# A causal convolution by fast algorithms on one core: H1's S rows stored in reverse, one F operation for H0, and two lists of steps in a new order

## The chip, the core and the metric

The kernel runs on one core of one Trainium2 chip. The metric is device microseconds (us) of one execution, the median of several runs; lower is better. A core has TensorE (matrix products, written PE in the profile), VectorE (DVE), ScalarE (ACT), GpSimd (POOL, which here also issues most loads) and SyncE (SP, which issues the stores and the transposing loads). The engines run their own lists of instructions in order and wait for each other through semaphores.

## What is computed

```python
def reference(x, kernel):          # x: 8 x 4096 x 512, kernel: 8 taps x 512 x 512, float32
    out = np.zeros_like(x)
    for k in range(8):
        shifted = x if k == 0 else np.concatenate([np.zeros((B, k, D)), x[:, :-k, :]], axis=1)
        out += np.matmul(shifted, kernel[k])
    return out
```

Each output row is the sum of eight products of the last eight input rows with eight 512 x 512 matrices.

## The kernel before

The 8 x 4096 rows are cut into 128 runs of 256 steps in time; the run is the partition, the step is the `t` of the code. Rows of `x` are loaded as bf16 and brought into a ring `XR` of 20 steps, with the 512 features on the partitions. The first four steps are done directly (`direct(tap, t)`, 32 products). The other 252 steps are 21 blocks of 12, and each block is done by a short convolution in two levels, which replaces products by sums of inputs and sums of weights. A block has four **nodes**, in this order: PL, MI, H1, H0. Node `n` counts from 1, so nodes 1 to 4 are the first block and node 84 is the last one. A "product" is four 128 x 128 by 128 x 512 matmuls.

A node that isn't a leaf (all but nodes 3 and 4) does this, and the names are the tokens of the order lists:

- `z`: seven rows `Z` (four for H0, which takes three over from H1), sums or differences of rows of `XR`, on DVE.
- `A`: two rows from `Z`, DVE. `s`: five rows `S` of sums of `Z` rows (four for H0), DVE. `F0`, `F1`: two rows each of `F`, sums of two `S` rows, for the two halves LO and HI, DVE.
- `a1`, `u`, `a0`: three products into the bank `q`, with a copy of `q` on ACT behind `a1`. `s0`, `s1`: ACT copies `q` into the banks of the two halves; `dt`: ACT copies the rest into the tile `DT`.
- `v0`, `v1`: one product of an `S` row into each half; `d0`, `d1`: DVE forms `DT - p` and `-p - DT` in the bank; `l00`, `l01`, `l10`, `l11`: four products of `F` rows.
- `e0`, `e1`: the half leaves PSUM into a tile `y` (pool of five) or is added to one: on ACT for PL, on DVE for the others. `ga`, `gb`, `ya`: sums of `y` tiles on POOL. `store` sends a `y` tile to DRAM through SP's queue, and a later `e` that takes the buffer waits until that store has landed.
- `x12`, `x16`, `x20`: transposing loads into `XR` (SP); `r0`, `r1`, `r2`: loads of later rows by POOL. `behind` ties a POOL operation to the DVE operation that was written last before it.

A node of H0 shares rows with H1. Its sums `S[1..4]` are written to rows 0 to 3, and `S[0]` is H1's last row, which still stands in row 4. So its two F operations read rows out of sequence: `F0` reads row 0 twice (a broadcast) and rows 1 and 4, `F1` rows 1 to 3.

The scheduler does nothing here (`manual_schedule`): each engine does its instructions in the order in which the code emits them. `ORDER` is the list for one block, a token `name.i` meaning step `name` of node `4m + i + 1` for block `m`: `.0` is PL, `.1` MI, `.2` H1, `.3` H0, `.4` and `.5` the next block's PL and MI. In front of it stands the set-up, written as some 190 calls: loads of the eight taps (`load_w`), direct products, transposes on PE (`transpose_pe`) for the first rows, filler matmuls on zeros (`fill`), the 28 sums of weights (`wsum(a, b, c)`, `plus`), each one DVE operation of 128 x 2048, and the steps of nodes 1 to 6 in an order of their own. `do` runs a step once only, so the loop over `ORDER` skips what the set-up has done.

```python
    W[a, b, c]                      # a: H1, H0, MI, PL = 0, 1, 2, 3; b, c: LO, HI, MID = 0, 1, 2
    load(W[n >> 2, n >> 1 & 1, n & 1], kr[:, :, tap, :])     # n = 7 - tap
```

In listings of instructions a weight tile reads `w211_91` for `W[MI, HI, HI]` and so on; `w3_96` is the tile of all PL weights, which first holds rows of `x`, and `w4_97` holds S and A rows of the first nodes.

Of the kernel before, what the change touches and what calls it, by code (L numbers as in the profile page):

```python
# [14 lines left out]
def kernel(  # L15
# [379 lines left out]
    def s_rows(n, a, b):  # L395
# [5 lines left out]
        d1.1 l01.1 l00.1 s.2 a0.2 x12.0 u.2 l10.1 e1.0 s0.2 e0.1 s1.2 l11.1 v0.2 z.3 F0.2 A.3 F1.2 ga0.2  # L401
        v1.2 x20.1 dt.2 a1.3 d0.2 r0.2 l01.2 e1.1 l00.2 s.3 a0.3 u.3 gb0.2 d1.2 e0.2 l10.2 E0.2 z.4 F0.3
        r1.2 A.4 l11.2 s1.3 F1.3 s0.3 v0.3 v1.3 ya0.2 r2.2 dt.3 d0.3 a1.4 l01.3 e1.2 l00.3 s.4 gb1.2 a0.4
        d1.3 e0.3 u.4 l11.3 z.5 s0.4 F0.4 A.5 s1.4 dt.4 ga1.2 v0.4 v1.4 l10.3 d0.4 a1.5 d1.4 l00.4 l01.4
        a0.5 u.5 e0.4 F1.4 e1.3 s.5 s0.5 l10.4 dt.5 s1.5 z.6 A.6 x16.4 l11.4 F0.5 v0.5 v1.5 a1.6 d0.5 F1.5
# [38 lines left out]
    nc.vector.memset(zero, 0.0)
    nc.sync.dma_start(out=XF, in_=xr[:, 0:4, :])
    cast(nc.vector.tensor_copy, 2, 4)
    make_identity(nc, ident)
    for k in range(7):
        fill(pair(2 + k % 2))
    rows(H[:, 4:8], RUN - 4, 4)  # L450
    cast(nc.scalar.copy, 0, 2)
    transpose_pe("x0", 2, xin[0], 0, 4)
    load_w(0)
    load_w(4)
    fill(pair(3))
    fill(pair(3))
    here(nc.scalar.copy, 0, "x0", 0, 2)
    transpose_pe("h4", 3, H, 4, 8)
    here(nc.scalar.copy, 0, "x0", 2, 4)
    fill(pair(2))  # L460
    history(nc.scalar.copy, -4, "h4")
    direct(0, 1)
    go(3, "v0")
    go(2, "d1")
    direct(0, 0)
    direct(0, 2)
    direct(0, 3)
    direct(4, 2)
    fill(pair(2))
    load_w(1)  # L470
    direct(4, 0)
    direct(1, 1)
    direct(1, 3)
    wsum(MI, HI, HI)
    load_w(5)
    load_w(3)
    wsum(MI, HI, LO)
    direct(1, 0)
    load_w(7)
    direct(5, 3)  # L480
    plus((HI, LO))
    wsum(MI, HI, MID)
    go(3, "F1")
    plus((HI, HI))
    plus((LO, LO))
    wsum(PL, HI, MID)
    rows(H[:, 1:4], RUN - 7, 3)
    load_w(6)
    direct(1, 2)
    direct(4, 1)  # L490
    wsum(H1, MID, LO)
    direct(3, 0)
    direct(4, 3)
    direct(3, 3)
    load_w(2)
    load_xin(4)
    direct(5, 1)
    direct(3, 1)
    wsum(H0, MID, LO)
    wsum(PL, MID, LO)  # L500
    transpose_pe("h3", 2, H, 1, 4)
    load_xin(8, 0, 2)
    go(4, "F1")
    direct(7, 3)
    wsum(MI, LO, LO)
    history(nc.scalar.copy, -7, "h3")
    direct(6, 3)
    wsum(H0, MID, HI)
    plus((LO, HI))
    direct(3, 2)  # L510
    direct(6, 2)
    direct(5, 2)
    direct(5, 0)
    direct(2, 1)
    wsum(MI, LO, HI)
    transpose_pe("x4", 3, xin[4], 0, 4)
    wsum(PL, MID, HI)
    transpose_pe("x8", 2, xin[8], 0, 2)
    direct(7, 0)
    here(nc.scalar.copy, 4, "x4", 0, 2)  # L520
    wsum(MI, LO, MID)
    wsum(PL, LO, MID)
    wsum(MI, MID, HI)
    load_xin(8, 2, 4)
    direct(2, 0)
    here(nc.scalar.copy, 8, "x8", 0, 2)
    go(3, "d1")
    wsum(PL, MID, MID)
    direct(7, 1)
    here(nc.scalar.copy, 4, "x4", 2, 4)  # L530
    fill(pair(3))
    z_rows(nodes[1], 0, 5)
    node_A(nodes[1])
    load_x(12)
    transpose_pe("x9", 2, xin[8], 2, 4)
    direct(2, 3)
    here(nc.scalar.copy, 10, "x9", 0, 2)
    s_rows(nodes[1], 0, 3)
    direct(6, 0)
    z_rows(nodes[1], 5, 7)  # L540
    node_a1(nodes[1])
    load_x(16)
    wsum(H1, MID, HI)
    s_rows(nodes[1], 3, 5)
    direct(6, 1)
    go(2, "v1")
    fill(pair(2))
    node_u(nodes[1])
    node_z(nodes[2])
    node_a0(nodes[1])  # L550
    go(1, "F1")
    node_A(nodes[2])
    direct_out(0)
    node_dts(nodes[1])
    direct(7, 2)
    node_seed(nodes[1], 0)
    node_seed(nodes[1], 1)
    wsum(MI, MID, LO)
    node_F(nodes[1], 0)
    for t in range(20, 40, 4):  # L560
        load_x(t)
    direct(2, 2)
    node_v(nodes[1], 0)
    node_d(nodes[1], 0)
    go(2, "F0")
    wsum(MI, MID, MID)
    node_a1(nodes[2])
    go(1, "s")
    node_v(nodes[1], 1)
    direct_out(1)  # L570
    go(1, "l01")
    go(1, "l00")
    node_d(nodes[1], 1)
    go(1, "e0")
    go(1, "u")
    go(1, "a0")
    transpose_x(12)
    go(1, "l10")
    go(1, "z")
    do("x16", 1)  # L580
    go(1, "l11")
    go(1, "s1")
    wsum(H1, MID, MID)
    go(1, "s0")
    go(1, "v0")
    go(1, "dt")
    go(1, "F0")
    go(1, "A")
    go(1, "d0")
    go(1, "a1")  # L590
    go(2, "F1")
    go(1, "v1")
    go(2, "l01")
    go(2, "l00")
    go(2, "a0")
    go(2, "u")
    go(1, "e1")
    go(1, "d1")
    go(2, "s0")
    go(2, "dt")  # L600
    wsum(H0, MID, MID)
    go(3, "dt")
    go(2, "s")
    go(3, "v1")
    go(2, "e0")
    go(2, "l11")
    go(2, "z")
# [95 lines left out]
```

## Time and profile before

| | |
|---|---|
| median of 3 runs (lowest, highest) | 718.1 us (717.59, 718.16) |
| span of the profiled execution | 717.2 us; the page has no other time of its own for it, so it stands 0.9 below the median |
| PE busy | 696.0 us (97%), 3205 records of matmuls |
| DVE busy | 683.3 us (95%), 767 instructions |
| ACT, POOL busy | 287.7 us (40%), 167.5 us (23%) |
| granted PE clock | 0.998 of full |
| DMA | 138.86 MB, mean 194 GB/s |

Busy time counts the union of an engine's instructions. DVE's instructions overlap by some 0.08 us (the next one starts before the recorded end of the last), so the price of one in a packed row is the distance of two starts, not its recorded duration. The same holds for matmuls of PE: recorded 379 ns, but 0.216 us apart.

### The profile page before, as it was taken

What the parts mean: (1) busy time and instruction counts of PE and PEld (TensorE: products, weight loads), DVE (VectorE), ACT (ScalarE), POOL (GpSimd) and SP (SyncE); (2) the same over time, 40 slices, a digit from 0 to 9 for tenths busy, and PEclk for the clock granted to TensorE, in tenths of its full rate; (3) what the DMA queues carried; (4) which work ended last, traced back from release to release, by engine and by line L of the source; (5) the groups of instructions that cost most, each with busy time, mean ns of one, the idle gap of its engine ahead of it and who ended that gap; (6) DMA issues with size and microseconds to landing.
All of it is one profiled execution on the core that took longest, in us unless ns stands there. A gap on an engine that the chain in (4) does not pass through costs nothing.

```text
span 717.2 us, 8960 instructions
## 1 busy us (share of the span) xinstructions
PE 696.0 (97%) x3205; PEld 315.0 (44%) x3270; DVE 683.3 (95%) x767; ACT 287.7 (40%) x448; POOL 167.5 (23%) x180
## 2 busy tenths in 40 slices
PE   7989999999999999999999999999999999999995
PEld 3444444444444444444444444444444444444442
DVE  1899999999999999999999999999999999999994
ACT  3043244343435444343443434353443434444341
POOL 4200012213131221304122131312213041221212
PEclk9999999999999999999999999999999999999999
DMA  9996988788797878879788887977788698855414
GB/s 194 209 225 139 235 156 243 158 233 181 206 226 174 233 167 231 181 189 217 182 241 158 231 184 205 229 176 229 168 237 174 189 224 178 238 119 186 157 68 175
DMA packets 159515, 138.86 MB, mean 194 GB/s; under 512 B 130160, under 2 KB 134256, under 8 KB 159344
## 3 DMA queue, kind: packets, MB, share of 16 engines
q1 hardware_dynamic: 145312, 99.37, 46.6%
q0 software_dynamic: 13728, 38.15, 31.6%
q10 hardware_dynamic: 432, 0.79, 0.3%
...
q14 instruction: 18, 0.15, 0.1%
HBM read 77.33 MB, written 99.09 MB: 246 GB/s over the span
## 4 chain that ended last, share of the span: by engine, by line
PE 84%; DVE 5%; issue 5%; DMA 0%; POOL 0%; DVEq 0%; POOLq 0%
PE pp L127 84%; DVE w L84 2%; DVE Z L84 2%; DVE y L87 1%; DVE S L84 1%; DMA out_dram<-y 0%; POOL y L311 0%; DVE y L84 0%; DVE F L84 0%; DVE pp L87 0%; DVE pp L84 0%; POOL xd L93 0%; DVEq L84 0%; DVEq L87 0%; POOLq L93 0%
## 5 line engine op out<-in xcount | busy, mean ns | idle before, releaser
L127 PE MATMUL pp<-w,F 128*128 128x512 bf16 x1285 | 310.4, 379 | 3.2 <-DVE pp L87 1.3
L127 PE MATMUL pp<-w,Z 128*128 128x512 bf16 x941 | 231.9, 379 | 2.7 <-DVE Z L84 1.7
L127 PEld LDWEIGHTS <-F 128*128 128x128 bf16 x1312 | 128.3, 98 | 157.6 <-issue 3.4
L311 POOL TENSOR_TENSOR y<-y 128x512 f32<-128x512 f32 x80 | 101.7, 1272 | 406.0 <-DVE F L84 266.1
L127 PE MATMUL pp<-w,S 128*128 128x512 bf16 x658 | 157.5, 379 | 0.7
L84 DVE TENSOR_TENSOR Z<-XR 128x2048 bf16<-128x2048 bf16 (+3 forms) x109 | 154.5, 1435 | 2.5
L127 PEld LDWEIGHTS <-Z 128*128 128x128 bf16 x960 | 92.3, 98 | 118.2 <-DVE Z L84 9.4
L198 ACT COPY pp<-pp 128x512 f32<-128x512 f32 x82 | 46.7, 570 | 221.1 <-PE pp L127 221.1
L84 DVE TENSOR_TENSOR S<-Z 128x2560 bf16<-128x2560 bf16 (+1 forms) x81 | 114.5, 1413 | 0.0
L84 DVE TENSOR_TENSOR F<-S 128x1024 bf16<-128x1024 bf16 x160 | 111.1, 694 | 1.9 <-PE pp L127 1.9
L127 PEld LDWEIGHTS <-S 128*128 128x128 bf16 x672 | 65.8, 98 | 79.4 <-issue 0.2
L214 ACT COPY pp<-pp 128x512 f32<-128x512 f32 (+1 forms) x84 | 48.9, 582 | 76.5 <-PE pp L127 76.5
...
L84 DVE TENSOR_TENSOR pp<-DT,pp 128x512 f32<-128x512 f32 x82 | 56.3, 687 | 0.2 <-PE pp L127 0.2
L87 DVE SCALAR_TENSOR_TENSOR pp<-pp,DT 128x512 f32<-128x512 f32 x82 | 56.5, 689 | 0.0
L216 ACT ACTIVATE pp<-pp 128x512 f32<-128x512 f32 (+1 forms) x84 | 50.1, 596 | 15.2 <-PE pp L127 9.8
L84 DVE TENSOR_TENSOR Z<-Z 128x1024 bf16<-128x1024 bf16 x78 | 53.4, 684 | 0.7
L87 DVE SCALAR_TENSOR_TENSOR y<-pp,y 128x1024 f32<-128x1024 f32 x42 | 51.0, 1215 | 0.0
L220 ACT COPY DT<-pp 128x512 f32<-128x512 f32 x82 | 48.9, 597 | 2.6 <-PE pp L127 2.6
L268 ACT COPY y<-pp 128x1024 f32<-128x1024 f32 x40 | 40.6, 1016 | 22.9 <-PE pp L127 21.7
L87 DVE SCALAR_TENSOR_TENSOR y<-y,pp 128x1024 f32<-128x1024 f32 (+1 forms) x41 | 48.3, 1181 | 0.3 <-PE pp L127 0.3
L270 ACT ACTIVATE y<-y 128x1024 f32<-128x1024 f32 x40 | 42.3, 1057 | 2.8 <-DMA out_dram<-y 0.6
...
## 6 DMA issues: line engine op xcount, KB each, us to landing
...
XR<-xd SPq DMA_TRANSPOSE x61, 4.8
...
```

The lines of the kernel that those rows point to most:

```text
L84: last["dve"] = nc.vector.tensor_tensor(out=o, in0=a, in1=b, op=op)
L87: last["dve"] = nc.vector.scalar_tensor_tensor(out=o, in0=a, scalar=by, in1=b, op0=MUL, op1=op)
L93: return nc.gpsimd.dma_start(out=o, in_=src)
L127: nc.tensor.matmul(bank, lhsT=comp[:, c * P:(c + 1) * P], rhs=w[:, c, :], start=start and c == 0, stop=c == DC - 1, skip_group_check=True)
L198: nc.scalar.copy(out=n.q[:, 0], in_=n.q[:, 1])
L214: nc.scalar.copy(out=o, in_=q)
L216: nc.scalar.mul(out=o, in_=q, mul=-1.0)
L220: nc.scalar.copy(out=DT, in_=n.q[:, 0])
L268: nc.scalar.copy(out=cc[b_], in_=p)
L270: nc.scalar.mul(out=dd[b_], in_=cc[b_], mul=-0.5)
L311: behind(nc.gpsimd.tensor_tensor(out=cc[b_][:, j], in0=cc[b_][:, j], in1=dd[b_][:, j], op=ADD), b_ > j and n.k)
```

## The change

- A node of H1 that isn't a leaf writes its five `S` rows in reverse (`n.s[:, ::-1]`), so its first sum lies in row 4 and its last in row 0. H0 now writes its four sums to rows 1 to 4, and `S[0]`, H1's last, stands in row 0: its five rows lie in sequence.
- `F0` and `F1` of H0 become one operation `F` of four rows. `comps` names the rows that the products read, so that each product reads what it read before.
- The list `ORDER` is written anew, and the set-up is one list of tokens, `SETUP`, that reaches to node 9 and has the loads, sums, fillers and steps in a new order. The count of matmuls is as before (3168 of 128 x 512 for the products, 26 fillers, 76 transposes); DVE has 21 instructions fewer.

```diff
     def node_s(n):
+        z, o = n.z, n.o
         if n.shares:
-            tt(n.s[:, 0:4], n.z[:, n.o + 1:n.o + 5], n.z[:, n.o + 3:n.o + 7], ADD)
+            tt(n.s[:, 1:5], z[:, o + 1:o + 5], z[:, o + 3:o + 7], ADD)
+        elif n.rev:
+            tt(n.s[:, ::-1], z[:, o:o + 5], z[:, o + 2:o + 7], ADD)
...
-    def node_F(n, b_):
+    def node_F(n, b_=None):
         if n.leaf:
             return
-        s, f = n.s, F[:, 2 * b_:2 * b_ + 2]
-        if not n.shares:
-            tt(f, s[:, 2 * b_:2 * b_ + 2], s[:, 2 * b_ + 1:2 * b_ + 3], ADD)
-        elif b_ == LO:
-            tt(f, s[:, 0:1].to_broadcast([P, 2, D]), s[:, 1:5:3], ADD)
-        else:
-            tt(f, s[:, 1:3], s[:, 2:4], ADD)
+        n.whole = b_ is None
+        a, b = (0, 4) if n.whole else (2 * b_, 2 * b_ + 2)
+        i = 2 - a if n.rev and not n.whole else a
+        tt(F[:, a:b], n.s[:, i:i + b - a], n.s[:, i + 1:i + 1 + b - a], ADD)
...
     ORDER = """
...
-        r1.2 A.4 l11.2 s1.3 F1.3 s0.3 v0.3 v1.3 ya0.2 r2.2 dt.3 d0.3 a1.4 l01.3 e1.2 l00.3 s.4 gb1.2 a0.4
...
+        l11.2 z.4 A.4 dt.3 v0.3 F.3 d0.3 r1.2 v1.3 a1.4 l01.3 s.4 l00.3 a0.4 u.4 ya0.2 e1.2 s0.4 gb1.2 d1.3
...
+    SETUP = """
+        zero f3 f3 f3 f3 X0 k2 f3 w0 H4 f2 f2 id k0 f2 f2 w4 w1 tx0 cx0a cx0b f2 f2 D02 w5 D01 D03 th4 D00
+        ch4 p311 s211 p310 D40 D42 D11 w3 w7 s312 D13 D10 D53 D41 D30 H3 s210 w6 s212 D12 D51 w2 D31 D43
+        s012 X8 p300 D33 D73 th3 s120 X4 s320 X9 L12 D63 L20 s020 D32 s021 ch3 s200 D62 p301 L16 D50 s201
...
+    """.split()
...
+    for token in SETUP:
+        act(token)
```

In `SETUP`, `f` is a filler, `w5` the load of tap 5, `D53` `direct(5, 3)`, `s211` the sum for `W[MI, HI, HI]`, `p311` the sum of two for `W[PL, HI, HI]`, `tx4` a transpose on PE and `cx4a` its copy on ACT, `L12` a load of later rows.

**DVE in the set-up.** These are the first rows behind the cast of the first input rows; `w111_83` and `w011_75` are taps 0 and 4, `w110_82` and `w010_74` taps 1 and 5, `w100_80` and `w000_71` taps 3 and 7. Before:

```order
L370 MEMSET XR_98 128x128
L84 TENSOR_TENSOR w211_91<-w111_83,w011_75 128x2048
L84 TENSOR_TENSOR w210_90<-w110_82,w010_74 128x2048
L84 TENSOR_TENSOR w3_96<-w110_82,w010_74 128x2048
L84 TENSOR_TENSOR w212_92<-w210_90,w211_91 128x2048
L84 TENSOR_TENSOR w3_96<-w111_83,w011_75 128x2048
L84 TENSOR_TENSOR w3_96<-w100_80,w000_71 128x2048
```

Now:

```order
L374 MEMSET XR_98 128x128
L84 TENSOR_TENSOR w3_96<-w111_83,w011_75 128x2048
L84 TENSOR_TENSOR w211_91<-w111_83,w011_75 128x2048
L84 TENSOR_TENSOR w3_96<-w110_82,w010_74 128x2048
L84 TENSOR_TENSOR w3_96<-w3_96 128x2048
L84 TENSOR_TENSOR w210_90<-w110_82,w010_74 128x2048
L84 TENSOR_TENSOR w212_92<-w210_90,w211_91 128x2048
L84 TENSOR_TENSOR w012_76<-w010_74,w011_75 128x2048
L84 TENSOR_TENSOR w3_96<-w100_80,w000_71 128x2048
```

Two sums that need taps 0 and 4 alone now stand ahead of the first that needs tap 5, where one stood; and five rows, where three and one of the earlier ones stood, lie between those and the first row that needs taps 3 and 7: `w012_76` has come forward from much later.

**DVE in a block.** These rows reach from H1's half sum `e0` (y 128x512) over H0 to H0's `e0` in the third block. `pp_1109` and `pp_1089` are H0's LO half, `pp_1039` and `pp_1053` H1's HI half. Before:

```order
L84 TENSOR_TENSOR y<-pp_1036,y 128x512
L84 TENSOR_TENSOR Z<-XR 128x3584
L84 TENSOR_TENSOR F<-S 128x1024
L84 TENSOR_TENSOR Z<-Z 128x1024
L84 TENSOR_TENSOR F<-S 128x1024
L84 TENSOR_TENSOR pp_1109<-DT,pp_1109 128x512
L84 TENSOR_TENSOR y<-pp_1039,y 128x1024
L84 TENSOR_TENSOR S<-Z 128x2560
L87 SCALAR_TENSOR_TENSOR pp_1106<-pp_1106,DT 128x512
L87 SCALAR_TENSOR_TENSOR y<-y,pp_1109 128x1024
```

Now:

```order
L84 TENSOR_TENSOR y<-pp_1030,y 128x512
L84 TENSOR_TENSOR Z<-XR 128x3584
L84 TENSOR_TENSOR Z<-Z 128x1024
L84 TENSOR_TENSOR F<-S 128x2048
L84 TENSOR_TENSOR pp_1089<-DT,pp_1089 128x512
L84 TENSOR_TENSOR S<-Z 128x2560
L84 TENSOR_TENSOR y<-pp_1053,y 128x1024
L87 SCALAR_TENSOR_TENSOR pp_1098<-pp_1098,DT 128x512
L87 SCALAR_TENSOR_TENSOR y<-y,pp_1089 128x1024
```

The two F rows are one of 128x2048 behind the A row, and H1's `e1` (y 128x1024 from H1's HI half) now stands behind the next node's S row, not ahead of it.

**POOL at the start.** `w111_83<-in_kernel_dram` is tap 0, `w3_96<-in_x_dram` the rows before the start of each run (`H4`), `ident` the matrix for PE's transposes. Before:

```order
masks.py:197 MEMSET ident_103 128x128
masks.py:199 ISA
masks.py:199 AFFINE_SELECT ident_103<-ident_103 128x128
L93 DMA w3_96<-in_x_dram 128x2048
L93 DMA w111_83<-in_kernel_dram 128x4x512
L93 DMA w011_75<-in_kernel_dram 128x4x512
```

Now:

```order
L93 DMA w111_83<-in_kernel_dram 128x4x512
L93 DMA w3_96<-in_x_dram 128x2048
masks.py:197 MEMSET ident_103 128x128
masks.py:199 ISA
masks.py:199 AFFINE_SELECT ident_103<-ident_103 128x128
L93 DMA w011_75<-in_kernel_dram 128x4x512
```

Tap 0 and `H4` have changed places, and both are issued ahead of the matrix `ident`.

More of the change, by code (lines that the diff above doesn't have):

```diff
@@ L136, in __init__ @@
             self.shares = a == H0 and not self.leaf
+            self.rev = a == H1 and not self.leaf
+            self.whole = False
             self.s = WX[:, 0:5] if k <= EARLY and k % 2 else S
@@ L400 @@
     ORDER = """
[L401 to L405 removed]
+        d1.1 e1.0 l01.1 s.2 l00.1 a0.2 u.2 s0.2 e0.1 l10.1 z.3 F0.2 l11.1 A.3 F1.2 dt.2 x12.0 v0.2 x20.1
+        ga0.2 s1.2 a1.3 r0.2 v1.2 d0.2 l01.2 l00.2 e1.1 s.3 a0.3 gb0.2 u.3 d1.2 s0.3 l10.2 e0.2 E0.2 s1.3
+        l11.2 z.4 A.4 dt.3 v0.3 F.3 d0.3 r1.2 v1.3 a1.4 l01.3 s.4 l00.3 a0.4 u.4 ya0.2 e1.2 s0.4 gb1.2 d1.3
+        l11.3 dt.4 e0.3 s1.4 z.5 l10.3 A.5 r2.2 ga1.2 v0.4 F0.4 v1.4 a1.5 d0.4 d1.4 F1.4 l00.4 l01.4 e0.4
+        a0.5 u.5 e1.3 s.5 z.6 l10.4 l11.4 dt.5 A.6 s0.5 v0.5 F0.5 s1.5 x16.4 v1.5 a1.6 d0.5 F1.5
     """.split()
@@ L438, in do @@
             ACTS[name](nodes[k])
-    def go(k, name):
-        do("a1" if name == "b1" else name, k + AHEAD.get(name, 0))
-    pd = {0: pair(0), 1: pair(1)}
[L444 to L607, printed above, removed]
-    do("x12", 1)
-    go(2, "l10")
-    go(3, "l00")
-    go(2, "s1")
-    go(2, "a1")
-    go(2, "A")
-    go(3, "l01")
-    go(3, "u")
-    go(2, "e1")
-    behind(load_x(48))
-    go(3, "s")
-    go(3, "z")
-    go(3, "l11")
-    go(3, "g0")
-    go(4, "g1")
-    wsum(H1, LO, MID)
@@ L624 @@
-    go(3, "a0")
-    wsum(H1, HI, MID)
-    go(2, "v0")
-    go(3, "F0")
-    do("x20", 1)
-    go(3, "e0")
-    go(3, "s0")
-    go(3, "A")
-    go(3, "l10")
-    go(3, "e1")
-    go(2, "d0")
-    go(4, "l01")
-    go(3, "s1")
-    go(4, "l00")
-    behind(load_x(40))
-    go(4, "b1")
-    go(4, "l10")
-    behind(load_x(44))
-    go(4, "s")
-    go(4, "u")
-    go(4, "e0")
-    go(4, "s1")
-    go(4, "s0")
-    go(4, "l11")
-    go(4, "z")
-    go(4, "F0")
-    go(4, "A")
-    go(4, "a0")
-    go(4, "dt")
@@ L653 @@
-    go(3, "d0")
-    go(4, "e1")
-    go(4, "v0")
-    go(4, "v1")
-    go(4, "a1")
-    go(4, "d0")
-    go(4, "d1")
+    PE_T = {"x0": (2, xin[0], 0, 4), "h4": (3, H, 4, 8), "h3": (2, H, 1, 4), "x4": (3, xin[4], 0, 4),
+            "x8": (2, xin[8], 0, 2), "x9": (2, xin[8], 2, 4)}
+    BITS = (LO, HI, MID)
+    FIRST = {
+        "zero": lambda: nc.vector.memset(zero, 0.0),
+        "X0": lambda: nc.sync.dma_start(out=XF, in_=xr[:, 0:4, :]),
+        "k2": lambda: cast(nc.vector.tensor_copy, 2, 4), "k0": lambda: cast(nc.scalar.copy, 0, 2),
+        "id": lambda: make_identity(nc, ident),
+        "H4": lambda: rows(H[:, 4:8], RUN - 4, 4), "H3": lambda: rows(H[:, 1:4], RUN - 7, 3),
+        "X4": lambda: load_xin(4), "X8": lambda: load_xin(8, 0, 2), "X9": lambda: load_xin(8, 2, 4),
+        "ch4": lambda: history(nc.scalar.copy, -4, "h4"), "ch3": lambda: history(nc.scalar.copy, -7, "h3"),
+    }
@@ new lines, with act @@
+    """.split()
+    def act(token):
+        name, _, k = token.partition(".")
+        if token in FIRST:
+            FIRST[token]()
+        elif k:
+            if name in PARTS:
+                done.add((name[0], int(k)))
+                PARTS[name](nodes[int(k)])
+            else:
+                do(name, int(k))
+        elif name.startswith("out"):
+            direct_out(int(name[3:]))
+        elif name[0] == "f":
+            fill(pair(int(name[1:])))
+        elif name[0] == "w":
+            load_w(int(name[1:]))
+        elif name[0] == "T":
+            transpose_x(int(name[1:]))
+        elif name[0] == "L":
+            load_x(int(name[1:]))
+        elif name[0] == "B":
+            behind(load_x(int(name[1:])))
+        elif name[0] == "t":
+            p = PE_T[name[1:]]
+            transpose_pe(name[1:], *p)
+        elif name[0] == "c":
+            t, h = int(name[2:3]), name[3:]
+            lo = 0 if h == "a" else 2
+            src = "x" + str(t)
+            here(nc.scalar.copy, {0: 0, 4: 4, 8: 8, 9: 10}[t], src, lo, lo + 2)
+        elif name[0] == "D":
+            direct(int(name[1]), int(name[2]))
+        elif name[0] in "sp":
+            a, b_, c_ = (int(i) for i in name[1:])
+            if name[0] == "p":
+                plus((b_, c_))
+            else:
+                wsum(a, b_, c_)
```

27 lines of the change are left out of this document (21 added, 6 removed).

## Prediction

> **What bounds the kernel now.** I read the page first, then the busy time by stage, then the instructions in order of time at each place where PE loses time.
>
> ```profile
> span 717.2 us, 8960 instructions
> PE 696.0 (97%) x3205; PEld 315.0 (44%) x3270; DVE 683.3 (95%) x767; ACT 287.7 (40%) x448; POOL 167.5 (23%) x180
> PE 84%; DVE 5%; issue 5%; DMA 0%; POOL 0%; DVEq 0%; POOLq 0%
> ```
>
> PE carries 84% of the chain of work that ended last, and DVE is nearly as full. By stage (us, then PE, weight loads, DVE, ACT, POOL busy, clock, DMA share, GB/s):
>
> ```profile
> 26.00:53.10 27.10, 23.61 (x139) 11.51 (x140) 26.97 (x28) 9.66 (x12) 3.09 (x6) 1.00 1.10 218
> 53.10:119.00 65.90, 65.22 (x295) 29.22 (x301) 65.75 (x69) 24.49 (x37) 8.22 (x11) 1.00 0.84 184
> 119.00:300.00 181.00, 180.10 (x820) 81.47 (x837) 178.38 (x204) 77.19 (x123) 45.83 (x47) 1.00 0.80 202
> 300.00:310.00 10.00, 8.59 (x39) 3.72 (x39) 10.00 (x11) 2.23 (x4) 2.55 (x2) 1.00 0.91 246
> 551.00:560.00 9.00, 7.65 (x34) 3.23 (x34) 9.00 (x11) 2.23 (x4) 2.54 (x2) 1.00 0.94 251
> ```
>
> From 119 to 300 PE is busy for 99.5%: that is its ceiling in this view. It loses 3.5 us from 26 to 53 while DVE is full, about 0.35 us more than that ceiling allows from 53 to 119, and some 1.3 us at each of two short places in the middle. So there are three sorts of time: the set-up, two stalls, and a long stretch where PE sets the pace and only a shortfall of another engine can be felt.
>
> How near that shortfall is: prices from one packed stretch, as the distance of starts.
>
> ```profile
> 204.16 0.69 DVE L84 TENSOR_TENSOR pp<-DT,pp 128x512 f32<-128x512 f32 x1
> 204.76 1.22 DVE L84 TENSOR_TENSOR y<-pp,y 128x1024 f32<-128x1024 f32 x1
> 205.90 1.48 DVE L84 TENSOR_TENSOR S<-Z 128x2560 bf16<-128x2560 bf16 x1
> 207.30 0.69 DVE L87 SCALAR_TENSOR_TENSOR pp<-pp,DT 128x512 f32<-128x512 f32 x1
> 209.03 2.02 DVE L84 TENSOR_TENSOR Z<-XR 128x3584 bf16<-128x3584 bf16 x1
> 210.96 0.68 DVE L84 TENSOR_TENSOR F<-S 128x1024 bf16<-128x1024 bf16 x1
> 224.38 1.21 DVE L84 TENSOR_TENSOR Z<-XR 128x2048 bf16<-128x2048 bf16 x1
> 225.52 0.68 DVE L84 TENSOR_TENSOR F<-S 128x1024 bf16<-128x1024 bf16 x1
> ```
>
> Two rows (or one f32 row of PSUM) cost 0.60 us, four 1.14, five 1.40, seven 1.93, a full `y` 1.14. One block on DVE is 20 of the small ones (12.0), S 3 x 1.40 + 1.14 (5.3), Z 3 x 1.93 + 1.14 (6.9) and `y` 5 x 1.14 + 0.60 (6.3): 30.5 us. On PE:
>
> ```profile
> 218.36 1.89 PE L127 MATMUL pp<-w,S 128*128 128x512 bf16 x8
> 220.08 1.03 PE L127 MATMUL pp<-w,Z 128*128 128x512 bf16 x4
> ```
>
> Eight matmuls take 1.72 us of starts, so a product is 0.863 and a block of 36 products is 31.08 us. DVE has half a microsecond to spare in each block.
>
> **The change, part by part.**
>
> *Set-up, DVE.* Here are its first weight sums and the start of the first Z:
>
> ```profile
> 14.87 1.23 DVE L84 TENSOR_TENSOR w<-w,w 128x2048 bf16<-128x2048 bf16 x1 [1.77 <-DMA w<-in_kernel_dram]
> 19.95 4.63 DVE L84 TENSOR_TENSOR w<-w,w 128x2048 bf16<-128x2048 bf16 x4 [3.86 <-DMA w<-in_kernel_dram]
> 25.79 1.23 DVE L84 TENSOR_TENSOR w<-w,w 128x2048 bf16<-128x2048 bf16 x1 [1.21 <-DMA w<-in_kernel_dram]
> 42.02 1.48 DVE L84 TENSOR_TENSOR Z<-XR 128x2560 bf16<-128x2560 bf16 x1
> ```
>
> DVE waits 3.86 us for tap 5 and 1.21 us for tap 7, and from 25.79 it is packed. Nineteen sums stand ahead of the first Z in both versions, but now a second one fills the first wait and `w012` the second. Two sums at 1.14 us less to do after 25.79: the first Z at 42.02 - 2.3 = 39.7, if no later sum waits for its tap. The order now takes tap 6 after twelve sums (25.8 + 4 x 1.14 = 30.3) and tap 2 after two more (32.6). The loads that were queued behind taps 7, 6 and 2 start when they have landed:
>
> ```profile
> 25.98 0.53 POOL L93 DMA_DIRECT2D xd<-in_x_dram x1 [1.95 <-DMA w<-in_kernel_dram]
> 30.35 0.52 POOL L93 DMA_DIRECT2D xd<-in_x_dram x1 [2.02 <-DMA w<-in_kernel_dram]
> 32.89 0.52 POOL L93 DMA_DIRECT2D xd<-in_x_dram x1 [2.02 <-DMA w<-in_kernel_dram]
> ```
>
> Tap 6 by 30.35 and tap 2 by 32.89 cost nothing or 0.2 us. The exchange of tap 0 and `H4` moves DVE's first memset (and the sums behind it) to about 16: `H4` lands third, its transposes and a copy follow. Two sums end by 18.3, ahead of 19.95, so that is hidden; if tap 0 as the first load delays the first inputs, PE's own wait for those rows (its other products end near 14.6) takes up 1.3 us of it.
>
> *Set-up, PE.* What PE waits for at the end of the direct products:
>
> ```profile
> 36.36 0.45 PEld L357 LDWEIGHTS <-w 128*128 128x128 bf16 x8 [0.19 <-DMA w<-in_x_dram]
> 44.28 1.04 PE L127 MATMUL pp<-w,w 128*128 128x512 bf16 x4 [2.10 <-DVE w L84]
> 53.09 1.89 PE L127 MATMUL pp<-w,F 128*128 128x512 bf16 x7 [0.43 <-DVE pp L84]
> ```
>
> At 44.28 `a1` of node 1 waits 2.10 us for the A row. Now A follows Z by 1.42 + 0.60 + 0.60 and is done at 42.3. PE: rows 4 to 7 of `x` are now the second of the two loads that end at 36.36; behind them come 16 and 8 transposes (0.06 each, by the first row: 1.5 us), five direct products (4.3) and two filler matmuls (0.4), so PE is there at 42.6. Three direct products are left in both. `a1` starts 1.65 us earlier, and PE is no longer the one that waits. Up to the first product of F (53.09) the running sums of DVE and PE stay within 0.2 us of each other, against 0.43 and smaller waits before: 51.0, a gain of 2.1.
>
> From there to 119 both versions keep PE and DVE packed, and the lead has to survive that. I laid the two running sums of the new order side by side: at some ten products the operand is ready only 0.0 to 0.2 us ahead (`l11` of node 2, `a1` of nodes 4 and 6, `l01` of nodes 6 and 7). Before, PE lost 0.35 us there. I take 2.0 us for the set-up; the bounds are 0.5 (each of those places costs what 53.09 cost, 0.43 us, in three or four cases) and 2.6 (no wait is left).
>
> *The two stalls.* This is the DVE operation in front of each, the store that it waits for, and PE behind it:
>
> ```profile
> 299.97 1.22 DVE L84 TENSOR_TENSOR y<-pp,y 128x1024 f32<-128x1024 f32 x1 [1.59 <-DMA out_dram<-y]
> 303.25 1.02 PE L127 MATMUL pp<-w,F 128*128 128x512 bf16 x4 [0.71 <-DVE pp L87]
> 307.52 1.04 PE L127 MATMUL pp<-w,Z 128*128 128x512 bf16 x4 [0.64 <-DVE Z L84]
> 550.66 1.23 DVE L84 TENSOR_TENSOR y<-pp,y 128x1024 f32<-128x1024 f32 x1 [1.40 <-DMA out_dram<-y]
> L253 SPq DMA_DIRECT2D out_dram<-y x1: 333/333/333, 294.0 to 294.0; - x1
> DMA to landing us min/median/max: 5.8/5.8/5.8
> ```
>
> It is `e1` of H1: its `y` buffer is the one whose store went out about 4.3 us before `e1`'s turn. In the block that starts near 200 that store landed in 3.3 us; in two of 20 it took 5.7 to 5.8, DVE stood 1.59 and 1.40 us, and PE lost 1.35 and about 1.3 (551 to 560). In the new order the store's POOL operations hang on the same DVE row (H0's S), but `e1` comes after Z, A, F of four, d and S of five: two F operations (1.20) are gone from that stretch, 1.14 + 1.40 are in it, so it is 1.34 us later. The waits shrink to 0.25 and 0.06, which DVE's spare time covers. Gain 2.5; bounds 0 (such a delay meets another store) and 2.65.
>
> *The F operation.* 1.14 for 2 x 0.60: DVE saves 0.06 us a block, 1.2 in all, where PE sets the pace: nothing. `F` now waits for `l11` of H1 as a whole, so H0's `d0` comes 1.8 us after that product, as before within 0.1 us, and `l01` starts two products plus `a1` (2.6) after it. Later `e1` frees its bank later for `s0` of the next PL, and `l10` has moved between `u` and `v0` to make up for it (1.1 us ahead, 0.24 before). No wait in a block: cost 0.
>
> *S in reverse.* The trace has no negative step. Nearest row: Z and S at 2560 elements, 1.40; F of H0 with a broadcast row and a row step of three costs 0.68 recorded, like the plain ones, so I take 1.40. The upper bound is one element per cycle: five rows from 1.40 to 2.73, the difference of 2560 elements at the slope of the rows above (1.40 - 0.60 for 1536, 0.52 ns each). The Trainium skill (Vector Engine (DVE) Microarchitecture Reference, 5.1 Performance modes) gives two results per cycle to 2-byte operands whose innermost step is +1 or -1, which a reversed order of whole rows keeps, and says that an operand with a negative step has not been measured; by that rule the sum stays as it is.
>
> *The end.* In the last block nothing stands between these rows:
>
> ```profile
> 704.56 0.69 DVE L84 TENSOR_TENSOR F<-S 128x1024 bf16<-128x1024 bf16 x1 [1.93 <-PE pp L127]
> 705.50 0.70 DVE L84 TENSOR_TENSOR pp<-DT,pp 128x512 f32<-128x512 f32 x1 [0.24 <-PE pp L127]
> 706.24 3.62 PE L127 MATMUL pp<-w,F 128*128 128x512 bf16 x15
> ```
>
> F of four ends its turn at 704.56 + 1.14 = 705.70, `d0` starts 0.2 us later than at 705.50, and so does PE's last run: +0.2 (0 to 0.3).
>
> Sum: 717.2 - 2.0 - 2.5 + 0.2 = 712.9 for the profiled execution; the median of the runs stands 0.9 above its span, so 713.8.
>
> **The rivals.**
>
> *The stalls stay or move* to another wait on a store. For it: I can't say what delays a store to 5.8 us every 251 us, and five buffers are shared by all halves. Against it: apart from those two, this is the longest wait for a store in the trace:
>
> ```profile
> ACT y L270 <- DMA out_dram<-y: 0.6, 1, 0.6
> ```
>
> That gives 717.2 - 2.0 + 0.2 + 0.9 = 716.3.
>
> *The lead of the set-up is lost* in the packed stretch to 119, where DVE has no idle time to absorb a delay: at the lower bound, 0.5, it gives 718.1 - 0.5 - 2.5 + 0.2 = 715.3; at nothing 715.8. With both rivals at once 718 remains.
>
> *S in reverse at half rate.* From 0.5 us of slack on, every block pays: 1.33 - 0.5 = 0.8, over 20 blocks 17 us: 731. Slower.
>
> *A store that ACT waits for.* POOL's `ya` hangs on the S of the next PL now, 2 us later, and the store of H1's LO half goes out behind it, 7.5 us before ACT's copy of the next PL needs that buffer (17.5 by DVE's running sum in a block, against the end of the 29th product, 25.0). The neighbouring stores have needed this:
>
> ```profile
> DMA to landing us min/median/max: 4.6/6.7/8.8
> ```
>
> (the two stores issued at 236.9 and 237.3). This store was the quick one, and a load that slowed the other has moved 4 us away. If it took 8.5 in every block, ACT would be 1.0 us late, with 0.3 to spare ahead of `v0`: 0.6 x 20 = 13 us, so 727. Slower.
>
> **How the numbers follow.** The forecast has 0.58, stalls that stay 0.15, a lost lead 0.12, both 0.05, the reversed S 0.04, the store for ACT 0.06. Predicted: 713.8. Its own range is 712.2 (every term at its better bound) to 715.5. The range for 8 in 10 reaches over the first two rivals: 712.2 to 717.4, leaving out both together and the two slower ones (0.15) and a little below. A difference of 0.2% (1.4 us) is about what measurements of this kernel can tell from no change. Faster: the forecast and most of the first two rivals, 0.80; same: what of these stays above 716.7, and both together, 0.10; slower 0.10.
>
> **What would show it.** Right: DVE packed from 20 on, `a1` of node 1 near 42.6 and the first F product near 51; no wait of DVE over 0.3 us on a store; S of H1 recorded at 1.48; one F of 1.21 in each block; PE at its ceiling from 119 on. Wrong: a wait of PE that returns in every block, S of H1 near 2.8, ACT waiting for a store ahead of its copies, or a first Z at 42 as before.

## The result, and the profile after

The changed kernel took 723.7 us (median of 6 runs, 723.0 to 728.7) against 717.7 for the kernel before (6 runs, 716.9 to 718.2): ratio 1.0093, 95% interval 1.0075 to 1.0111. Forecast were 713.8 us, at most 717.4. It is slower where faster was expected, and the sign of the sum is wrong, not only a size. The profiled execution took 723.0 us with a span of 721.2, 4.0 us over the span of before.

Page of the changed kernel: span, busy time, and the chain of work that ended last.

```profile
span 721.2 us, 9024 instructions
PE 704.3 (98%) x3270; PEld 313.9 (44%) x3270; DVE 688.7 (95%) x747; ACT 286.6 (40%) x448; POOL 169.9 (24%) x180
DVE 58%; PE 15%; issue 10%; POOL 1%; DMA 0%; POOLq 0%; DVEq 0%
```

Before, PE carried 84% of the chain and DVE 5%. Now DVE carries 58%. PE's busy share does not show this, since its waits are short and return in each block. DVE has 20 instructions fewer and yet is busy 5.4 us longer, so some of its rows must have become longer. They are found where the same shape has a longer record than elsewhere. First before, DVE and then POOL, about the F1 of PL in one block:

```profile
306.77 0.68 DVE L84 TENSOR_TENSOR Z<-Z 128x1024 bf16<-128x1024 bf16 x1
308.58 0.78 DVE L84 TENSOR_TENSOR F<-S 128x1024 bf16<-128x1024 bf16 x1
309.28 1.21 DVE L87 SCALAR_TENSOR_TENSOR y<-y,pp 128x1024 f32<-128x1024 f32 x1
...
307.54 1.27 POOL L311 TENSOR_TENSOR y<-y 128x512 f32<-128x512 f32 x1 [3.58 <-DVE Z L84]
```

The same place after:

```profile
308.40 0.69 DVE L84 TENSOR_TENSOR Z<-Z 128x1024 bf16<-128x1024 bf16 x1
309.01 0.68 DVE L84 TENSOR_TENSOR F<-S 128x1024 bf16<-128x1024 bf16 x1
310.81 0.96 DVE L84 TENSOR_TENSOR F<-S 128x1024 bf16<-128x1024 bf16 x1
311.70 1.21 DVE L87 SCALAR_TENSOR_TENSOR y<-y,pp 128x1024 f32<-128x1024 f32 x1
...
309.39 0.54 POOL L93 DMA_DIRECT2D xd<-in_x_dram  x1 [3.09 <-DVE Z L84]
309.94 1.28 POOL L315 TENSOR_TENSOR y<-y 128x512 f32<-128x512 f32 x1
```

The POOL sum is `ga1`. Both it and the load ahead of it (`r2`) are tied to the A that ends at 309.09. In the new list `r2` stands right ahead of `ga1` on POOL's queue, so the sum starts at 309.94 and ends at 311.22; before, it started 0.09 us after the A (307.45 and 307.54). F1 reads and writes no `y` tile. Yet F1 ends 0.55 us after the sum's end in both versions (308.81 and 309.36; 311.22 and 311.77), and it is recorded as work, not as idle time. A free F is 0.68.

What follows is in the starts of the `y` rows of H0, which come twice per block (`e0`, then `e1`): before 114.50, 120.66, 145.58, after 116.55, 123.03, 147.99. From `e0` to `e1` the 6.17 us have become 6.48, in all of 17 blocks (0.31 x 17 = 5.3 us); from `e1` to the next `e0` it is 24.9 us in both. From 651 on, where no more rows are loaded, the short part is 6.26 and 6.19. The account of the 4.0 us: +2.05 already at 116.55, +5.3 in the blocks, -3.2 for the two waits on a store, which are gone, -0.1 in small differences between blocks and at the end.

The 2.05 us of the set-up. PE, ACT, and the first rows of DVE:

```profile
1.20 6.84 PE L355 MATMUL pp<-DT 128*128 128x512 bf16 x18 [1.20 <-DVE DT L446]
11.26 2.08 PE L355 MATMUL pp<-DT 128*128 128x512 bf16 x4 [2.01 <-ACT XR L377]
16.45 1.06 PE L361 MATMUL pp<-ident,w 128*128 128x128 bf16 x16
17.54 1.85 ACT L373 COPY XR<-pp 128x2032 bf16<-128x2032 bf16 x1 [6.33 <-PE pp L361]
19.70 1.41 DVE L84 TENSOR_TENSOR w<-w,w 128x2048 bf16<-128x2048 bf16 x1 [13.52 <-issue]
19.89 0.17 DVE L374 MEMSET XR<- 128x128 bf16 x1
42.81 2.09 DVE L84 TENSOR_TENSOR Z<-XR 128x2560 bf16<-128x2560 bf16 x2
```

DVE's first weight sum starts at 19.70, not 14.87. It stands in DVE's list behind the clearing of the history rows' columns (recorded at 19.89), which waits for ACT's copy, which waits for the transposes at 16.45. These stand behind 18 filler matmuls (14 before), the transposes of `x0`, four more fillers that wait 2.01 us for a bank, and three direct products. PE also runs most of these fillers and products at half its clock. This is PE's busy time, its matmuls, granted clock and DMA in one stretch, first before and then after:

```profile
11.20:14.50 3.30, 2.23 (x11) 1.00 1.24 206
11.20:14.50 3.30, 3.19 (x8) 0.50 1.22 203
```

The trace of the changed kernel grants half the clock from 11.17 to 14.59. The sixteen matmuls from 11.26 to 16.45 take 5.19 us; at 0.216 each it would be 3.46, so by this estimate 1.7 us of the late first sum come from the clock. The six kernels with this start (the changed one and runs 1, 2, 4, 8 and 14) all have such a stretch of 3.41 us, behind a wait of PE of 2.0 us; none of the other ten has one in its first 40 us. What makes the clock fall is not shown.

The new order of the sums makes up most of the delay: the first `d0` is 0.5 us late (52.83 and 52.35). Later in the set-up three POOL sums run back to back, and three rows of DVE beside them are 0.5 to 0.7 us over their usual records (F 0.68, S of H0 1.21, Z 2.02), 1.6 us together; against the kernel before, the stretch from this `d0` to the next is 1.1 us longer:

```profile
104.00 5.15 POOL L315 TENSOR_TENSOR y<-y 128x512 f32<-128x512 f32 x3 [3.97 <-DVE y L87]
104.43 1.39 DVE L84 TENSOR_TENSOR F<-S 128x1024 bf16<-128x1024 bf16 x1
106.34 1.68 DVE L84 TENSOR_TENSOR S<-Z 128x2048 bf16<-128x2048 bf16 x1
108.55 2.49 DVE L84 TENSOR_TENSOR Z<-XR 128x3584 bf16<-128x3584 bf16 x1
```

### The profile page after: what moved, and what is told of

Read it like the earlier page. It is cut to its first block, busy times and chain, and to the rows that moved or that the text cites. A ratio compares the mean times of both kernels' runs of the same rounds, so it can differ in the third digit from the quotient of the medians.

```text
span 721.2 us, 9024 instructions
## 1 busy us (share of the span) xinstructions
PE 704.3 (98%) x3270; PEld 313.9 (44%) x3270; DVE 688.7 (95%) x747; ACT 286.6 (40%) x448; POOL 169.9 (24%) x180
## 4 chain that ended last, share of the span: by engine, by line
DVE 58%; PE 15%; issue 10%; POOL 1%; DMA 0%; POOLq 0%; DVEq 0%
DVE Z L84 19%; PE pp L127 15%; DVE S L84 11%; DVE F L84 9%; DVE y L87 9%; DVE pp L84 3%; DVE y L84 3%; DVE pp L87 3%; DMA out_dram<-y 0%; POOL y L307 0%; POOL y L315 0%; POOLq L555 0%; DVEq L84 0%; POOLq L315 0%; POOLq L307 0%
## 5 line engine op out<-in xcount | busy, mean ns | idle before, releaser
L315 POOL TENSOR_TENSOR y<-y 128x512 f32<-128x512 f32 x80 | 103.8, 1299 | 296.0 <-DVE F L84 266.6
L127 PE MATMUL pp<-w,S 128*128 128x512 bf16 x672 | 162.0, 379 | 0.0
L84 DVE TENSOR_TENSOR Z<-XR 128x2048 bf16<-128x2048 bf16 (+3 forms) x109 | 156.5, 1454 | 1.1
L84 DVE TENSOR_TENSOR F<-S 128x1024 bf16<-128x1024 bf16 (+1 forms) x140 | 111.9, 799 | 2.5 <-PE pp L127 2.5
```

Source lines behind the costliest of these rows:

```text
L84: last["dve"] = nc.vector.tensor_tensor(out=o, in0=a, in1=b, op=op)
L127: nc.tensor.matmul(bank, lhsT=comp[:, c * P:(c + 1) * P], rhs=w[:, c, :], start=start and c == 0, stop=c == DC - 1, skip_group_check=True)
L315: behind(nc.gpsimd.tensor_tensor(out=cc[b_][:, j], in0=cc[b_][:, j], in1=dd[b_][:, j], op=ADD), b_ > j and n.k)
```

## The experiments

Theory A: DVE sets the pace, because POOL's sums hold its bf16 operations and because an A now starts later behind its Z; the set-up is late because of its first twenty steps, not because of the new order of sums. The rivals are named with each run. The kernel before had medians of 717.6 to 718.4 us beside these runs.

| run | us | ratio to before, 95% interval |
|---|---|---|
| 1 changed kernel, load `r2` moved behind `gb1` | 719.0 | 1.0014 (0.9999 to 1.0028) |
| 2 new set-up, old list | 724.9 | 1.0098 (1.0071 to 1.0125) |
| 3 old set-up, new list | 721.9 | 1.0051 (1.0035 to 1.0068) |
| 4 changed kernel, history rows first | 721.9 | 1.0053 (1.0035 to 1.0072) |
| 5 run 1 with the old start of the set-up | 714.4 | 0.9941 (0.9922 to 0.9961) |
| 6 run 3 with the load moved | 717.1 | 0.9982 (0.9972 to 0.9993) |
| 7 kernel before, load late | 729.5 | 1.0155 (1.0136 to 1.0175) |
| 8 changed kernel, F0 of PL between Z and A of MI | 732.6 | 1.0206 (1.0178 to 1.0233) |
| 9 kernel before, `e1` of H1 late | 730.1 | 1.0171 (1.0156 to 1.0187) |
| 10 run 5, `e1` of H1 early | 733.8 | 1.0222 (1.0206 to 1.0237) |
| 11 run 5, two F (one node twice) | 715.8 | 0.9970 (0.9958 to 0.9981) |
| 12 run 5, POOL sums of the set-up moved | 716.6 | 0.9990 (0.9973 to 1.0007) |
| 13 run 5, two F | 713.4 | 0.9943 (0.9927 to 0.9960) |
| 14 changed kernel, two F | 722.9 | 1.0075 (1.0060 to 1.0090) |

**Run 1: the load's issue.**

```
- ... e1.2 s0.4 gb1.2 d1.3 ... A.5 r2.2 ga1.2 v0.4 ...
+ ... e1.2 s0.4 gb1.2 r2.2 d1.3 ... A.5 ga1.2 v0.4 ...
```

> The changed kernel with one token moved: the issue of the third row load of a block stands behind the Pool sum of `gb1` instead of right ahead of `ga1`. Theory A (DVE has become the pace-setter; the load's issue makes `ga1` start 0.55 us later, and the bf16 F1 of PL that comes after it is held until `ga1` is done: 0.97 us recorded instead of 0.69): F1 of PL back to 0.69, block 31.43 -> 31.14 us, 17 blocks x 0.29 = 4.9 us, about 718.8. Rival B (PE's new order of products in the block, `a1` ahead of `v1` and `l10` ahead of `v0`, is what costs): nothing changes, 723.7, block 31.43.

719.0 us, 4.7 less than the changed kernel. F1 of PL and the POOL rows about it:

```profile
306.06 1.21 DVE L87 SCALAR_TENSOR_TENSOR y<-y,pp 128x1024 f32<-128x1024 f32 x1
311.65 0.68 DVE L84 TENSOR_TENSOR F<-S 128x1024 bf16<-128x1024 bf16 x1
312.25 1.21 DVE L87 SCALAR_TENSOR_TENSOR y<-y,pp 128x1024 f32<-128x1024 f32 x1
...
305.87 1.27 POOL L315 TENSOR_TENSOR y<-y 128x512 f32<-128x512 f32 x1
307.08 0.54 POOL L93 DMA_DIRECT2D xd<-in_x_dram  x1
310.01 1.64 POOL L315 TENSOR_TENSOR y<-y 128x512 f32<-128x512 f32 x1 [2.39 <-DVE Z L84]
```

The sum ends at 311.65 and F1 is free: 0.68, the short part of a block 6.19 again, PE back at 81% of the chain. Every product stands where the changed kernel has it, so rival B falls. (The sum is now recorded 1.64 instead of 1.27: it starts at 310.01 while the F0 of 309.85 to 310.53 runs, so here POOL is the one held.)

**Runs 2 and 3: one half of the change each.** Run 2 is the changed kernel with the loop list of before (the F's of H0 in two operations), run 3 the changed kernel with the set-up of before.

> New set-up, with the loop list of before (F of H0 in two operations again, S of H1 still in reverse). Theory A (the set-up is 2.05 us late by 116.55, whatever the list): block 31.08 to 31.15 again; 717.7 + 2.0 = 719.7 if the two waits for a `y` store come back, 716.7 if the other phase of the stores spares them. Rival C (the set-up costs nothing by itself; the 2 us at its end belong to the loop list, whose first block is in it): 717.7, or 714.7 without the waits.

> Set-up of before, with the new loop list, the F of four rows and S in reverse. Theory A: block 31.43 for some 16 blocks, 16 x 0.33 = 5.3 us lost, the two waits for a store gone (3.1 won): 717.7 + 5.3 - 3.1 = 719.9. Rival C (the list is harmless, and all the loss is from the set-up): 714.6.

Run 3: 721.9, 2 us over what A gave. The short part of a block is 6.48 as in the changed kernel, and the blocks start at 114.73, 0.23 behind before's; 1.2 of the 2 us are a loss about 556 that did not go (26.18 us from `e1` to `e0` there, 25.02 in the changed kernel). So the list alone loses. Run 2 came out 5 us over. Its blocks are 6.17 and 24.92 as before, but it is 3.3 us late at 117.79, and the waits for a store have doubled (before: 3.0 us in 2):

```profile
DVE y L84 <- DMA out_dram<-y: 6.1, 4, 2.5
```

With the same list, other stores are late here than before. That this hangs on when the set-up lets the blocks start is inferred from these two traces, and what delays a store was not found.

**Run 4: the history rows first.**

```
- X0 k2 f3 w0 H4 f2 f2 id k0 ... cx0b f2 f2 D02 w5 D01 D03 th4 D00 ch4 p311 ...
+ X0 k2 f3 H4 w0 f2 f2 id k0 ... cx0b f2 f2 th4 ch4 D02 w5 D01 D03 D00 p311 ...
```

> The changed kernel with the history rows first: their load is issued ahead of tap 0, and their PE transposes and ACT copy stand ahead of the first tap-0 products, as in the set-up of before. Theory A (the first weight sum waits at 19.70 behind the clearing of the history's columns on DVE's queue, which waits for those transposes): first weight sum near 15, first Z 42.8 -> about 40, first F product 54.17 -> about 52, and since DVE is packed from there the whole gain of 2 to 2.5 us arrives: about 721.4. Rival C (the landing of the weights sets the set-up: tap 7 lands at 26.05 and the sums behind it are all that counts; or the loads of x that are issued only at 69 us): first Z stays near 42.8, 723.7.

721.9 us. The first weight sum starts at 17.24 and the first Z at 41.03, the blocks at 114.87 (before 114.50, changed kernel 116.55). Right for A, though only half of the way back to 14.9: the 18 fillers and the wait of the other four are still ahead.

**Run 5: the start of before, the rest new.** The load as in run 1, and:

```
- zero f3 f3 f3 f3 X0 k2 f3 w0 H4 f2 f2 id k0 f2 f2 w4 w1 tx0 cx0a cx0b f2 f2 D02 w5 D01 D03 th4 D00 ch4 p311 ...
+ zero X0 k2 f2 f3 f2 f3 f2 f3 f2 H4 w0 id k0 w4 w1 tx0 f3 f3 cx0a th4 cx0b f2 ch4 D02 w5 D01 D03 D00 p311 ...
```

> The changed kernel with the load's issue moved as in the first run, and with the first 20 steps of the set-up in the order of before (14 fill products instead of 18 ahead of the first transposes, the history rows' load first, their transposes ahead of tap 0); all weight sums stay in the new order. Theory A (the new order of the sums is good, the start ahead of it is what made the set-up late): first weight sum near 14.9 instead of 19.7 to 21.1, the two waits for taps 5 and 7 filled, first Z near 40, the loop 2 us earlier than before, no wait for a store: 718.2 - 2.0 - 3.4 + 0.3 = about 713. Rival C (the new order of the sums itself costs, by its later loads of x or by Pool sums that meet bf16 work of DVE near 105): no earlier than before at 114, about 715 to 717.

714.4 us, 0.5% under the kernel before. The first rows of DVE:

```profile
12.33 0.17 DVE L374 MEMSET XR<- 128x128 bf16 x1 [6.05 <-ACT XR L373]
13.74 2.36 DVE L84 TENSOR_TENSOR w<-w,w 128x2048 bf16<-128x2048 bf16 x2 [1.24 <-DMA w<-in_kernel_dram]
18.81 1.23 DVE L84 TENSOR_TENSOR w<-w,w 128x2048 bf16<-128x2048 bf16 x1 [2.71 <-DMA w<-in_kernel_dram]
39.22 2.09 DVE L84 TENSOR_TENSOR Z<-XR 128x2560 bf16<-128x2560 bf16 x2
```

Two sums in the wait for tap 5, Z at 39.22 against 42.02: this is the forecast's own mechanism, 2.8 us where it had 2.3. The first `d0` is 3.1 us earlier than before (49.24 and 52.35). At 113.13 only 1.4 us are left. From the `d0` at 100.41 to the next at 109.40 alone 1.1 us of the lead go: there the three rows beside the POOL sums have the same 1.39, 1.69 and 2.49. Another 0.4 is a wait for a store at 77.19. No wait for a store is in the blocks.

**Run 6: both repairs, the old set-up.** Run 3 with the load of run 1.

> Set-up of before, new loop list with the load's issue moved. Theory A: 721.9 of the same without the move, less 17 blocks x 0.29: 717.0; against before, the two waits for a store gone but for one of 1.2 at 556 (seen in the run with the old set-up): 718.2 - 3.4 + 1.2 + 0.7 = 716.7. Rival B (the new order of products costs as well): 718 or more.

717.1 us, 4.8 less than run 3, as A had it. Rival B asked for 718 or more.

**Run 7: the load late in the kernel before.**

```
- ... ya0.2 r2.2 dt.3 ... dt.4 ga1.2 v0.4 ...
+ ... ya0.2 dt.3 ... dt.4 r2.2 ga1.2 v0.4 ...
```

> The kernel before with that one issue moved the other way: right ahead of `ga1`, as in the change. Theory A: F1 of PL recorded 0.97 instead of 0.78, DVE's block 31.1 -> 31.27 or more, so DVE passes PE: 17 x 0.19 = 3.2 us, 721.4, perhaps 1 us less or more where the stores' waits change phase. Rival B: no change, 718.2.

729.5 us. The direction is A's, the dose is more than three times what I gave (11.0 us against 3.2): in the old list the A stands one F later, so `ga1` starts later against F1.

```profile
279.89 1.56 DVE L84 TENSOR_TENSOR F<-S 128x1024 bf16<-128x1024 bf16 x1
...
279.07 0.54 POOL L93 DMA_DIRECT2D xd<-in_x_dram  x1 [3.81 <-DVE Z L84]
279.62 1.28 POOL L311 TENSOR_TENSOR y<-y 128x512 f32<-128x512 f32 x1
```

The sum ends at 280.90 and F1 at 281.45, again 0.55 behind it. One token in a list that is otherwise the old one costs 0.78 us a block (6.17 to 6.95), 11 us in all.

**Run 8: F0 of PL back between Z and A.** The Z and the A are those of MI (`z.5`, `A.5`); the text on record calls them PL's.

```
- l11.3 dt.4 e0.3 s1.4 z.5 l10.3 A.5 r2.2 ga1.2 v0.4 F0.4 ...
+ l11.3 dt.4 e0.3 s1.4 z.5 F0.4 l10.3 A.5 r2.2 ga1.2 v0.4 ...
```

> The changed kernel with F0 of PL put back between the Z and the A of PL, as in the list of before; the load's issue stays late. Theory A (an A right behind its Z starts only when the Z has ended: a step of 2.05 instead of 1.93): 0.12 us per block less on DVE, which sets the pace: 31.43 -> 31.31, 17 x 0.12 = 2.0 us, 721.7. Rival D (the step of 2.05 is a wait for another engine, or PE's `a1` of PL, which now gets its A 0.5 us later, takes it back): 31.43 stays, 723.7 or more.

732.6 us instead of 721.7, a miss that speaks for the hold. The A comes 0.48 us later, `ga1` with it, and F1 is held to 1.56 as in run 7: +0.60 for 0.12 won, 0.48 x 17 = 8.2, and 8.9 were measured.

**Runs 9 and 10: `e1` of H1 and the store.** Run 9 moves it in the kernel before, run 10 moves it back in run 5.

```
- ... l01.3 e1.2 l00.3 s.4 gb1.2 ...
+ ... l01.3 l00.3 s.4 e1.2 gb1.2 ...
```

```
- ... l01.3 s.4 l00.3 a0.4 u.4 ya0.2 e1.2 s0.4 ...
+ ... l01.3 e1.2 s.4 l00.3 a0.4 u.4 ya0.2 s0.4 ...
```

> The kernel before with e1 of H1 moved behind S of PL, as the change has it, and nothing else. Theory A (the two waits of DVE for a `y` store, 1.59 and 1.5 us recorded, 3.3 us of the block starts, end when e1 asks 1.4 us later): 718.2 - 3.3 = 714.9. Rival E (the store lands as late relative to e1 in some other block, since all of the kernel moves with it): one wait of 1 to 2 us stays somewhere, 716 to 718.

> The fastest version so far (714.4) with e1 of H1 moved back ahead of S of PL. Theory A: waits for a `y` store come back in one to four blocks, 1 to 2.6 us each: 717 to 720. Rival E (the waits belong to the phase that the old set-up gives the stores): 714.4 as without.

Both came out some 15 us over. Run 9, DVE and POOL:

```profile
302.14 2.32 DVE L84 TENSOR_TENSOR S<-Z 128x2560 bf16<-128x2560 bf16 x1
...
301.85 1.27 POOL L303 TENSOR_TENSOR y<-y 128x512 f32<-128x512 f32 x1 [0.59 <-issue]
```

The wait for a store is gone in run 9 (none in 120 to 700 us), as A said. But S now starts beside the POOL sum `ya`, which ran beside the f32 `e1` before, and is held from 1.48 to 2.32: 0.85 us in all but one block. In run 10 no wait for a store came back either; DVE waits for the sum itself, since `ya` reads the tile that the next `e0` overwrites:

```profile
306.60 1.22 DVE L87 SCALAR_TENSOR_TENSOR y<-y,pp 128x1024 f32<-128x1024 f32 x1 [0.91 <-POOL y L307]
```

So the new place of `e1` and the new place of `ya` belong together; either alone costs more than the two stalls did. Run 10 does not decide on the stalls.

**Runs 11, 13 and 14: the merge of the F's alone.** Runs 11 and 13 in run 5's kernel, run 14 in the changed one; 13 and 14 also mark the F's of node 8, which the set-up makes whole, as done.

```
- l11.2 z.4 A.4 dt.3 v0.3 F.3 d0.3 ...
+ l11.2 z.4 F0.3 A.4 dt.3 v0.3 F1.3 d0.3 ...
```

> The fastest version so far with the F of H0 in two operations again, the first between the Z and the A of PL. On DVE the two cost 0.06 us more than the one, and the A no longer stands right behind its Z, 0.12 less: 0.06 us per block less. Theory A (PE sets the pace at 31.1, DVE's sixteenth of a microsecond is spare): 714.4, no difference. Rival F (the single F is what lets DVE keep pace): 715.5 or more.

> The fastest version (714.4) with the F of H0 in two operations, the first between the Z and the A of PL, each node's F made once. Theory A (one F saves 0.06 us of DVE a block, but the A then stands right behind its Z and starts 0.12 later): 24.95 -> 24.90 us in the long part of a block, 18 x 0.05 = 0.8 us, 713.6. Rival F (the single F lets DVE keep pace): 715 or more.

> The changed kernel with the merge alone undone. Theory A: block 31.43 -> 31.38, 17 x 0.05 = 0.9 us, 722.8, and F1 of PL stays held at 0.97. Rival F: 724.5 or more, a block of 31.49.

In run 11 the F's of node 8 are made a second time from other rows, so that it does not compute the convolution; its time (715.8) is no evidence on the merge. Run 13: 713.4, the lowest time, 0.6% under the kernel before; but that kernel itself was 0.8 us lower beside run 13 than beside run 5, so the times alone don't show a gain. Run 14: 722.9, where A had 722.8; its blocks start 1.5 us later than the changed kernel's (118.05), so here too the time alone is no proof. The blocks do show it: their long part is 24.90 us in both and 24.95 with the single F. The row that explains it, in run 13 and in the changed kernel:

```profile
272.65 0.69 DVE L84 TENSOR_TENSOR F<-S 128x1024 bf16<-128x1024 bf16 x1
273.25 0.69 DVE L84 TENSOR_TENSOR pp<-DT,pp 128x512 f32<-128x512 f32 x1
...
270.00 2.01 DVE L84 TENSOR_TENSOR Z<-XR 128x3584 bf16<-128x3584 bf16 x1
272.04 0.69 DVE L84 TENSOR_TENSOR Z<-Z 128x1024 bf16<-128x1024 bf16 x1
```

An operation that doesn't need the one ahead starts 0.09 us before that one's record ends (273.34, 273.25); an A behind its own Z starts 0.03 after it (272.01, 272.04). A Z takes 1.93 of starts with an F behind it, 2.04 to 2.06 with its A, where no POOL sum holds it. The single F saves 0.06 and makes one more such pair.

**Run 12: the POOL sums of the set-up.** `ga0` of node 7 goes behind the A of node 8, `gb0` behind its F, `gb1` behind the S of node 9. The text on record speaks of two of the three sums; the edit moves all three.

> The fastest version so far with two of the three Pool sums that stand back to back at 100.6 to 105.7 moved: the first starts behind the A of node 8, the other two go behind the F of node 8 and the S of node 9, beside f32 work of DVE. Theory A (a bf16 operation of DVE is held until a Pool sum that runs is done: F pair 1.39, S 1.69 and Z 2.49 us recorded there, 1.1 us over their usual times): some 0.5 to 1 us less at 113, and 713.6. Rival G (those three are slow for another reason): the same rows stay slow, 714.4.

716.6, slower than run 5, and rival G is out all the same:

```profile
100.91 0.68 DVE L84 TENSOR_TENSOR F<-S 128x1024 bf16<-128x1024 bf16 x1
102.11 1.21 DVE L84 TENSOR_TENSOR S<-Z 128x2048 bf16<-128x2048 bf16 x1
103.84 2.02 DVE L84 TENSOR_TENSOR Z<-XR 128x3584 bf16<-128x3584 bf16 x1
111.84 1.23 DVE L84 TENSOR_TENSOR y<-pp,y 128x1024 f32<-128x1024 f32 x1 [3.51 <-issue]
```

The held rows are back at their usual records, and DVE is 1.8 us ahead of run 5 at `d0` of node 8 (107.64 and 109.40). Then `e1` waits 3.5 us. A store of a middle tile was issued at 109.10 (105.77 in run 5), behind the POOL sum that was moved, and landed at 111.76, just ahead of `e1`'s start; that `e1` waited for its buffer is inferred from these times, the profile names no releaser.

## Why the prediction was wrong, step by step

*"DVE has half a microsecond to spare in each block"* is the step that failed first, and with it *"No wait in a block: cost 0"*. The 30.5 us were sums of free steps. DVE's own steps in a block of before add up to 31.0: F1 of PL is held by 0.10, and two pairs take 0.12 and 0.18 more (an A right behind its Z, a Z right behind an S). These are DVE's own and no waits on PE: in the changed kernel, where DVE carries 58% of the chain and PE 15%, the same places cost the same (S to Z: 1.58 before, 1.59 after). So the slack against PE's 31.08 was 0.1 us and not 0.5. Another place that looks alike is a wait on PE: the Z of PL starts 0.12 to 0.17 us late before, in each of 17 blocks 0.04 us behind the end of a PE product that reads a Z row. In the changed kernel that Z starts on time, but a POOL sum holds it (2.12 instead of 2.02), and this 0.10 and the 0.05 of the single F are more than the slack. The rest of the new cost came out in full: 0.19 for F1 of PL and 0.12 for the A of MI, which also stands right behind its Z now, 0.31 x 17 = 5.3 us. Together, 31.0 + 0.10 + 0.05 + 0.19 + 0.12, they give the 31.4 of a block in the changed kernel.

*The F operation* was costed by its duration and by `F`'s waits on PE. Its place on DVE was not: it takes the F from between the Z and the A. Measured by undoing it: a loss of 0.05 us a block, 0.8 us, where I had nothing.

*POOL's queue* is the term that was not in the sum. I looked at what `ya` and `e1` wait for, not at `r2`, which the new list moves from behind `ya` to right ahead of `ga1`; and I did not ask what runs on DVE while a POOL sum runs. By runs 1 and 6 that one place is worth 4.7 and 4.8 us. No rival had it.

*Set-up, DVE*: I wrote that the memset would move to about 16 and be hidden, since two sums would still end before 19.95. It came at 19.89. Mis-sized were the fillers ahead of `x0`'s transposes (18 instead of 14, PE at the transposes at 8.19 instead of 6.65), the four fillers that wait for a bank, and the three products ahead of the history transposes. The sum took PE at full clock here; the half clock, 1.7 us of it by the estimate above, was not in it. The mechanism behind it was right: in run 5 Z starts at 39.22, forecast 39.7. The step from there to 119, "I take 2.0", was too high even then: 1.4 arrived, and 1.1 were lost beside POOL's sums.

*The two stalls*: forecast 2.5, measured 3.2 at the `y` rows of the two blocks; right in sign, a quarter too small. Run 9 shows that `e1`'s later place ends these waits in the kernel before, and that it needs `ya` moved as well.

*S in reverse*: 1.481 us against 1.479 before (means of 42 from 150 to 590 us), as taken. *The end*: +0.1 at PE's last product, +0.2 at the end of the span; forecast 0.2.

Of the rivals, "the lead of the set-up is lost" came nearest, but it stopped at a lead of zero; the set-up was 2 us late. The other three are out: no wait for a store is left in the blocks, S of H1 is at its price, and ACT waits for no store in the changed kernel (the sum given for that rival, 0.6 x 20 = 13, is 12). Of the signs of being wrong, two came: a first Z at 42 as before (42.81), and "a wait of PE that returns in every block". Here is one such place, where a product of 0.863 is followed 1.17 us later:

```profile
285.83 1.03 PE L127 MATMUL pp<-w,Z 128*128 128x512 bf16 x4
287.00 1.89 PE L127 MATMUL pp<-w,F 128*128 128x512 bf16 x8
```

PE stands 0.3 us there, behind `d0` of MI, which a DVE without a gap reaches that much later than PE.
